# Ones-matmuls one slice later, attention tails in three steps, SGU steps strewn: one change to a hybrid decoder layer on eight NeuronCores

## The chip, the cores, the metric

One Trainium2 chip, all 8 cores. Cores 2b and 2b+1 compute sequence b of four: the even core its first 1116 positions, the odd core the other 932, for which it also builds keys and values of the first 1024 positions (the context stage). No core waits for another. SGU is the spatial gating unit, adaLN the conditioning by c. The metric is the device time of one execution in microseconds (us), that is of the slowest core.

Such a program has a second, slower state: one die (cores 0 to 3 or 4 to 7), or both, shows a lower granted TensorE clock. Slow runs are not compared here. Beside fast runs I use the spans of **odd cores on undisturbed dies**: dies whose two even cores both lie within 0.2% of the lowest even core of that kernel's runs.

## The reference, cut

```python
mod = silu(c) @ w_ada + b_ada                    # adaLN: shift, scale, gate, twice
h = rms(x, norm1_g) * (1 + scale1) + shift1
zu, zv, zq, zk, zvb, za, zb = split(h @ w_in)
y_a = gelu(zu) * (w_s @ rms(gelu(zv)) + b)       # SGU, in 128-position chunks, 16 groups
# y_b: 16 heads, two 128-wide q/k components each, v of 256
q, k = rms(q, q_norm_g), rms(k, k_norm_g)        # QK norm
p = softmax(q @ k.T * 128**-0.5 - slope * dist, causal)
o = (p[:, :, 0] - lam * p[:, :, 1]) @ v
y_b = rms(o, subln_g) * (1 - lambda_init)
x = x + gate1 * ((sigmoid(za) * y_a + sigmoid(zb) * y_b) @ w_out)
x = x + gate2 * conv_ffn(rms(x, norm2_g) * (1 + scale2) + shift2)
# ... shapes, spatial gating and ConvFFN cut
```

## The kernel before

The program of each engine is fixed when the kernel is built: `P.pe`, `P.act`, `P.dve`, `P.pool` and `P.op("sp", ...)` append to five lists, and semaphore waits follow from the buffers that are named. An engine executes its list in order, so what is emitted first is done first. A projection (`spec_F`, or `spec_T` for V) is a chain of groups of 32 accumulating matmuls, cut into four **slices** of eight; after each slice `bg.slice()` runs what was put off (`later`) and then, at a given rate, the next steps of attention and SGU.

```python
class Bg:
    def __init__(self):
        self.q, self.rate, self.credit, self.pend, self.now = deque(), 0.0, 0.0, deque(), 0
        self.gate, self.open = set(), True

    def slice(self):
        self.now += 1
        while self.pend and self.pend[0][0] <= self.now:
            self.pend.popleft()[1]()
        self.credit += self.rate
        while self.credit >= 1.0:
            self.credit -= 1.0
            if self.q:
                if self.gate and self.q[0] in self.gate and not self.open:
                    self.credit += 1.0
                    break
                self.q.popleft()()

    def later(self, fn, n=1):
        self.pend.append((self.now + n, fn))
# ...
def gemm(bk, m, n, lhs, rhs, rd, evict):

    for g in range(NG):
        P.pe([(lambda e, kc=kc, a=lhs(kc), b=rhs(kc): e.matmul(bk.v[0:m, 0:n], lhsT=a, rhs=b, start=(kc == 0), stop=(kc == FC - 1)))
              for kc in range(g * KS, (g + 1) * KS)], reads=rd(g), writes=[bk.b], acc=True)
        if g == NG - 1:
            evict(bk)
        yield
```

The QK norm: square the group's result on ScalarE, sum over partitions with a matmul by ones, then rsqrt (Ln, Exp) and scale. `later` with its default of 1 is reached in the very `bg.slice()` that follows the group, so the ones-matmul stands directly behind the group's last matmul. The sigmoids of the gates have a first and a second half too:

```python
def qknorm(sqr, tmr, gname, dst, dbuf):
    def ev(bk, n):
        q, _ = sqr.next()
        P.act(lambda e: e.activation(out=q.v[:, 0:n], in_=bk.v[:, 0:n], func=AF.Square), reads=[bk.b], writes=[q.b])

        def rest():
            sb = srow.next()
            P.pe(lambda e: e.matmul(sb.v[:, 0:n], lhsT=ones_b.v, rhs=q.v[:, 0:n], start=True, stop=True),
                 reads=[q.b, ones_b.b], writes=[sb.b])
            r, _ = tmr.next()
            ln_exp(sb.v[:, 0:n], r.v[:, 0:n], sb.b, r.b, 1.0 / 128)
            P.dve(lambda e: e.scalar_tensor_tensor(out=dst, in0=bk.v[:, 0:n], scalar=cc(gname), in1=r.v[:, 0:n], op0=ALU.mult, op1=ALU.mult),
                  reads=[bk.b, r.b, cst.b], writes=[dbuf], acc=True)
        bg.later(rest)
    return ev
# ...
def ev_sig(dst):
    def f(bk, l, r0, n):
        t, _ = tmr.next()
        tv = t.v[:, 0:n]
        P.act(lambda e: e.activation(out=tv, in_=bk.v[:, 0:n], func=AF.Exp, scale=-1.0), reads=[bk.b], writes=[t.b])
        P.dve(lambda e: e.tensor_scalar_min(out=tv, in0=tv, scalar1=EMAX), writes=[t.b])

        def rest():
            P.act(lambda e: e.activation(out=tv, in_=tv, func=AF.Ln, bias=onec, scale=1.0), reads=[cst.b], writes=[t.b])
            P.act(lambda e: e.activation(out=dst.v[:, l, r0 - OFF:r0 - OFF + n], in_=tv, func=AF.Exp, scale=-1.0),
                  reads=[t.b], writes=[dst.b], acc=True)
        bg.later(rest)
    return f
```

Attention of a head, in steps (**units**): for each pair of query block and key block `qk` (scores, exponential) and, `LAG` steps later, `pv` (accumulate P times V and the row sums in two banks, `acc`). After a block's last pair its tail (`tail1`), and four steps later the transposes (`tail2`):

```python
def qk(p, j, kb, nk):
    a, b = qcols[j]
    nq, kn = b - a, krows(kb)
    sb = srow.next()
    P.pe([(lambda e, cm=cm: e.matmul(sb.v[0:kn, cm * nq:(cm + 1) * nq], lhsT=K.v[:, cm, kb * 128:kb * 128 + kn],
                                     rhs=Q.v[:, cm, a - OFF:b - OFF], start=True, stop=True)) for cm in range(2)],
         reads=krd + [Q.b], writes=[sb.b])
    pt, _ = pTr.next()
    bi = h * c.NBMAX + (NC + j - kb)
    P.act(lambda e: e.activation(out=pt.v[0:kn, 0:2 * nq], in_=sb.v[0:kn, 0:2 * nq], func=AF.Exp, bias=cc("albi", bi)[0:kn], scale=SC),
          reads=[sb.b, cst.b], writes=[pt.b])
    if kb == nk - 1:
        o = a - blocks[j][0]
        P.dve(lambda e: e.tensor_tensor(out=pt.v[0:kn, 0:2 * nq].rearrange("p (a b) -> p a b", a=2),
                                        in0=pt.v[0:kn, 0:2 * nq].rearrange("p (a b) -> p a b", a=2),
                                        in1=tri[0:kn, None, o:o + nq].to_broadcast([kn, 2, nq]), op=ALU.mult),
              reads=[msk.b], writes=[pt.b])
    pts[p] = pt

def pv(p, j, kb, nk):
    a, b = qcols[j]
    nq, kn = b - a, krows(kb)
    pt = pts.pop(p)
    P.pe([(lambda e, cm=cm: e.matmul(acc[cm].v[0:nq, 0:257], lhsT=pt.v[0:kn, cm * nq:(cm + 1) * nq], rhs=V.v[0:kn, kb, 0:257],
                                     start=(kb == 0), stop=(kb == nk - 1))) for cm in range(2)],
         reads=vrd + [pt.b], writes=[acc[0].b, acc[1].b], acc=True)

ohs = {}

# ...
def tail1(j):
    nq = qcols[j][1] - qcols[j][0]
    oa, _ = oar.next()
    oh, _ = ohr.next()
    ohs[j] = oh
    x = j % 2
    rr, rs = sm_rr[x][0:nq], sm_rs[x][0:nq]
    P.act(lambda e: e.activation(out=oa.v[0:nq, 0, 0:257], in_=acc[0].v[0:nq, 0:257], func=AF.Copy), reads=[acc[0].b], writes=[oa.b])
    P.dve(lambda e: e.tensor_copy(out=oa.v[0:nq, 1, 0:257], in_=acc[1].v[0:nq, 0:257]), reads=[acc[1].b], writes=[oa.b])
    P.dve(lambda e: e.reciprocal(out=rr[:, :, None], in_=oa.v[0:nq, :, 256:257]), reads=[oa.b], writes=[B_rr[x]])
    P.dve(lambda e: e.tensor_scalar_mul(out=rr[:, 1:2], in0=rr[:, 1:2], scalar1=neglam.v[0:nq]),
          reads=[neglam.b], writes=[B_rr[x]])
    P.dve(lambda e: e.tensor_scalar_mul(out=oa.v[0:nq, 1, 0:256], in0=oa.v[0:nq, 1, 0:256], scalar1=rr[:, 1:2]),
          reads=[B_rr[x]], writes=[oa.b])
    P.dve(lambda e: e.scalar_tensor_tensor(out=oa.v[0:nq, 0, 0:256], in0=oa.v[0:nq, 0, 0:256], scalar=rr[:, 0:1], in1=oa.v[0:nq, 1, 0:256],
                                           op0=ALU.mult, op1=ALU.add), reads=[B_rr[x]], writes=[oa.b])
    P.act(lambda e: e.activation(out=jk.v[0:nq], in_=oa.v[0:nq, 0, 0:256], func=AF.Square, accum_out=rs), reads=[oa.b], writes=[jk.b, B_rs[x]])
    P.act(lambda e: e.activation(out=rs, in_=rs, func=AF.Ln, bias=epsc[0:nq], scale=1.0 / 256), reads=[cst.b], writes=[B_rs[x]])
    P.act(lambda e: e.activation(out=rs, in_=rs, func=AF.Exp, scale=-0.5), writes=[B_rs[x]])
    P.act(lambda e: e.activation(out=oh.v[0:nq, 0, :], in_=oa.v[0:nq, 0, 0:256], func=AF.Identity, scale=rs),
          reads=[oa.b, B_rs[x]], writes=[oh.b])
    P.dve(lambda e: e.scalar_tensor_tensor(out=oh.v[0:nq, 1, :], in0=oa.v[0:nq, 0, 0:256], scalar=rs, in1=oh.v[0:nq, 0, :],
                                           op0=ALU.mult, op1=ALU.subtract), reads=[oa.b, B_rs[x]], writes=[oh.b])

def tail2(j):
    a, b = qcols[j]
    nq = b - a
    oh = ohs.pop(j)
    sb = srow.next()
    P.pe([(lambda e, e2=e2, w=w: e.matmul(sb.v[:, e2 * nq:(e2 + 1) * nq], lhsT=oh.v[0:nq, w, e2 * 128:(e2 + 1) * 128], rhs=ident[0:nq, 0:nq],
                                          start=(w == 0), stop=(w == 1))) for e2 in range(2) for w in range(2)],
         reads=[oh.b, msk.b], writes=[sb.b])
    P.dve([(lambda e, e2=e2: e.tensor_scalar_mul(out=oT.v[:, e2, a - OFF:b - OFF], in0=sb.v[:, e2 * nq:(e2 + 1) * nq],
                                             scalar1=subc.v[:, e2:e2 + 1])) for e2 in range(2)],
          reads=[sb.b, subc.b], writes=[oT.b], acc=True)

for p, (j, kb, nk) in enumerate(pairs):
    ev[p].append(lambda p=p, j=j, kb=kb, nk=nk: qk(p, j, kb, nk))
    ev[p + LAG].append(lambda p=p, j=j, kb=kb, nk=nk: pv(p, j, kb, nk))
    if kb == nk - 1:
        ev[p + LAG].append(lambda j=j: tail1(j))
        ev[p + LAG + 4].append(lambda j=j: tail2(j))
out = []
for s in sorted(ev):
    out.append(lambda fs=ev[s]: [f() for f in fs])
return out
```

The loop over heads (scores, ones sums, tails and SGU take turns in three banks, `srow`; projections have three others, `mainb`):

```python
for h in range(H):
    last = h == H - 1
    load_sgu(h)
    if not last:
        load_ctx(h + 1)
    bg.rate = 0.0
    run(spec_F(("u", h), hb, hf.otiles, mainb, ev_u)); run_ada()
    bg.q.extend(attn_units(h))
    gated = sgu_units(h)
    bg.q.extend(gated)
    bg.gate, bg.open = set(gated), False
    if not last:
        bg.q.append(lambda h=h: y_unit(h))
    bg.spread(2 * NF + (0 if last else NF + NFK + NT_), 0.8 if last else 1.0)
    run(spec_F(("gb", h), hb, hf.otiles, mainb, ev_sig(sB))); run_ada()
    run(spec_F(("ga", h), hb, hf.otiles, mainb, ev_sig(sA)))
    bg.later(open_gate)
    if last:
        bg.flush_pend()
    run_ada()
    if not last:
        run(spec_F(("k", h + 1), hb, hf.xtiles, mainb, ev_qk(h + 1, "k"))); run_ada()
        run(spec_T(("v", h + 1), hb, blocks, mainb, ev_v(h + 1))); run_ada()
        run(spec_F(("q", h + 1), hb, hf.otiles, mainb, ev_qk(h + 1, "q"))); run_ada()
        bg.flush()
```

In the context stage of the odd cores, while keys and values of the context are projected, background steps load the core's own x and sum its squares; each loads what it uses itself (`own_build`, which normalises x in a second pass, does the same):

```python
def own_stat(ti, k0):
    (r0, n) = hf.xtiles[ti]
    xv, xb = xl1.load(osrc[ti], k0, n)
    for i in range(2):
        if k0 + i == 0:
            P.act(lambda e, i=i: e.activation(out=rst1[ti].v, in_=xv[i], func=AF.Square), reads=[xb[i]], writes=[rst1[ti].b])
        else:
            P.act(lambda e, i=i: e.activation(out=xv[i], in_=xv[i], func=AF.Square), writes=[xb[i]])
            P.pool(lambda e, i=i: e.tensor_tensor(out=rst1[ti].v, in0=rst1[ti].v, in1=xv[i], op=ALU.add), reads=[xb[i]], writes=[rst1[ti].b])
```

Of the kernel before, what the change touches and what calls it, by code (L numbers as in the profile page):

```python
# [78 lines left out]
class Prog:  # L79
# [12 lines left out]
    dsem = sem  # L92
# [272 lines left out]
def build(cfg):  # L365
# [20 lines left out]
    kT_s = scr("kT_s", [H, 128, 2, CMAX])  # L386
# [6 lines left out]
    with ExitStack() as st:  # L393
# [10 lines left out]
        def emit(P, hf):  # L404
            A = Arena(arena_t[:, :], AB)
            pb = [Bank(psum[i], i) for i in range(8)]
            bg = Bg()
            T, R, OFF, NC, NBLK, NKB = hf.T, hf.R, hf.OFF, hf.NC, hf.NBLK, hf.NKB
            blocks = [(128 * j, min(128, R - 128 * j)) for j in range(NBLK)]
            qcols = [(max(OFF, r0), r0 + n) for (r0, n) in blocks]  # L410
# [92 lines left out]
            def run(gen):  # L503
                for _ in gen:
# [6 lines left out]
                  reads=[cst.b], writes=[lamw.b])  # L511
# [170 lines left out]
# [10 lines that stand above are left out]
                        ln_exp(sb.v[:, 0:n], r.v[:, 0:n], sb.b, r.b, 1.0 / 128)  # L692
                        P.dve(lambda e: e.scalar_tensor_tensor(out=dst, in0=bk.v[:, 0:n], scalar=cc(gname), in1=r.v[:, 0:n], op0=ALU.mult, op1=ALU.mult),  # L693
                              reads=[bk.b, r.b, cst.b], writes=[dbuf], acc=True)
                    bg.later(rest)
                return ev

            Bkv_s = [[Buf(f"kv_s{h}.{i}") for i in range(4)] for h in range(H)]
            if NC:
                A.next_phase(off_h0 + FC * hf.C * 2)  # L700
                rst1 = [A.alloc(f"rso{i}", [128, n], F32) for i, (_, n) in enumerate(hf.xtiles)]
                kst = Ring(P, A, "kst", 2, [128, hf.C], BF16, dma=True)
                vst = Ring(P, A, "vst", 2, [128, NC // 2, 256], BF16, dma=True)
                sqb1 = Ring(P, A, "sqb", 1, [128, c.TW], BF16)
                tm1 = Ring(P, A, "tm", 1, [128, c.TW], F32)
                xl1 = XLoad("xo", 2, 2, max(n for _, n in hf.xtiles))
                h1 = HBuf("hown", hf.xtiles, R, TOP1)
                mainb = Banks(pb, [0, 1, 2, 3, 4])
# [11 lines that stand above are left out]
                def own_fin(ti):  # L720
                    n = hf.xtiles[ti][1]
                    sb = srow.next()
                    P.pe(lambda e: e.matmul(sb.v[:, 0:n], lhsT=ones_f.v, rhs=rst1[ti].v, start=True, stop=True),
                         reads=[rst1[ti].b, ones_f.b], writes=[sb.b])
                    ln_exp(sb.v[:, 0:n], rst1[ti].v, sb.b, rst1[ti].b, 1.0 / D)

                def own_build(ti, k0):
                    xv, xb = xl1.load(osrc[ti], k0, hf.xtiles[ti][1])
                    for i in range(2):
                        build_h(h1, ti, k0 + i, xv[i], xb[i], rst1[ti])  # L730
                for ti in range(len(hf.xtiles)):
                    for k0 in range(0, FC, 2):
                        bg.q.append(lambda ti=ti, k0=k0: own_stat(ti, k0))
                bg.q.append(lambda: None)
                for ti in range(len(hf.xtiles)):
                    bg.q.append(lambda ti=ti: own_fin(ti))
                for ti in range(len(hf.xtiles)):
                    for k0 in range(0, FC, 2):
                        bg.q.append(lambda ti=ti, k0=k0: own_build(ti, k0))
                bg.spread(int(0.8 * H * NG * (2 * len(hf.ctiles) + NC)))  # L740
                cblk = [(128 * j, 128) for j in range(NC)]

                def ctx_head(h):
                    cur = {}

                    def evk(bk, l, r0, n):
                        if r0 == 0:
                            cur[l] = kst.next()
                        t, s = cur[l]
                        qknorm(sqb1, tm1, "kg", t.v[:, r0:r0 + n], t.b)(bk, n)  # L750
                        if r0 + n == hf.C:
                            bg.later(lambda: P.op("sp", lambda e: e.dma_start(out=kT_s[h][:, l, 0:hf.C], in_=t.v), reads=[t.b], writes=[Bkv_s[h][l]], dsem=s))

                    def evv(bk, j, n):
                        hv = NC // 2
                        if j % hv == 0:
                            cur["v"] = vst.next()
                        t, s = cur["v"]
                        P.dve(lambda e: e.tensor_copy(out=t.v[:, j % hv, :], in_=bk.v[:, 0:256]), reads=[bk.b], writes=[t.b], acc=True)
                        if j % hv == hv - 1:  # L760
                            P.op("sp", lambda e: e.dma_start(out=vB_s[h][:, j - hv + 1:j + 1, :], in_=t.v), reads=[t.b],
                                 writes=[Bkv_s[h][2 + j // hv]], dsem=s)
                    run(spec_F(("kc", h), h0, hf.ctiles, mainb, evk))
                    run_ada()
                    run(spec_T(("vc", h), h0, cblk, mainb, evv))
                    run_ada()
                for h in range(H):
                    ctx_head(h)
                bg.flush()
                hb = h1  # L770
            else:
                hb = h0
# [107 lines left out]
            def ev_sig(dst):  # L880
                def f(bk, l, r0, n):
# [5 lines left out]
                    def rest():  # L887
                        P.act(lambda e: e.activation(out=tv, in_=tv, func=AF.Ln, bias=onec, scale=1.0), reads=[cst.b], writes=[t.b])
                        P.act(lambda e: e.activation(out=dst.v[:, l, r0 - OFF:r0 - OFF + n], in_=tv, func=AF.Exp, scale=-1.0),
                              reads=[t.b], writes=[dst.b], acc=True)  # L890
                    bg.later(rest)
                return f

            def attn_units(h):
# [1 line left out]
                K, Q, V = Ks[i], Qs[i], Vs[i]  # L896
                krd = [Kc[i][1]] + ([Kc[i][0]] if NC else [])
                vrd = [Vc[i][1], Vc[i][2]] + ([Vc[i][0]] if NC else [])
                LAG = 2
                ev = defaultdict(list)  # L900
                pts = {}
                pairs = []
# [33 lines left out]

                ohs = {}

                def tail1(j):
                    nq = qcols[j][1] - qcols[j][0]  # L940
                    oa, _ = oar.next()
                    oh, _ = ohr.next()
                    ohs[j] = oh
                    x = j % 2
                    rr, rs = sm_rr[x][0:nq], sm_rs[x][0:nq]
                    P.act(lambda e: e.activation(out=oa.v[0:nq, 0, 0:257], in_=acc[0].v[0:nq, 0:257], func=AF.Copy), reads=[acc[0].b], writes=[oa.b])  # L946
                    P.dve(lambda e: e.tensor_copy(out=oa.v[0:nq, 1, 0:257], in_=acc[1].v[0:nq, 0:257]), reads=[acc[1].b], writes=[oa.b])  # L947
                    P.dve(lambda e: e.reciprocal(out=rr[:, :, None], in_=oa.v[0:nq, :, 256:257]), reads=[oa.b], writes=[B_rr[x]])
# [3 lines left out]
                          reads=[B_rr[x]], writes=[oa.b])  # L952
                    P.dve(lambda e: e.scalar_tensor_tensor(out=oa.v[0:nq, 0, 0:256], in0=oa.v[0:nq, 0, 0:256], scalar=rr[:, 0:1], in1=oa.v[0:nq, 1, 0:256],  # L953
                                                           op0=ALU.mult, op1=ALU.add), reads=[B_rr[x]], writes=[oa.b])
                    P.act(lambda e: e.activation(out=jk.v[0:nq], in_=oa.v[0:nq, 0, 0:256], func=AF.Square, accum_out=rs), reads=[oa.b], writes=[jk.b, B_rs[x]])  # L955
                    P.act(lambda e: e.activation(out=rs, in_=rs, func=AF.Ln, bias=epsc[0:nq], scale=1.0 / 256), reads=[cst.b], writes=[B_rs[x]])
                    P.act(lambda e: e.activation(out=rs, in_=rs, func=AF.Exp, scale=-0.5), writes=[B_rs[x]])
# [2 lines left out]
                    P.dve(lambda e: e.scalar_tensor_tensor(out=oh.v[0:nq, 1, :], in0=oa.v[0:nq, 0, 0:256], scalar=rs, in1=oh.v[0:nq, 0, :],  # L960
                                                           op0=ALU.mult, op1=ALU.subtract), reads=[oa.b, B_rs[x]], writes=[oh.b])

                def tail2(j):
                    a, b = qcols[j]
                    nq = b - a
                    oh = ohs.pop(j)
# [8 lines left out]
                for p, (j, kb, nk) in enumerate(pairs):  # L975
                    ev[p].append(lambda p=p, j=j, kb=kb, nk=nk: qk(p, j, kb, nk))
                    ev[p + LAG].append(lambda p=p, j=j, kb=kb, nk=nk: pv(p, j, kb, nk))
                    if kb == nk - 1:
                        ev[p + LAG].append(lambda j=j: tail1(j))
                        ev[p + LAG + 4].append(lambda j=j: tail2(j))  # L980
                out = []
                for s in sorted(ev):
                    out.append(lambda fs=ev[s]: [f() for f in fs])
# [71 lines left out]
            for h in range(H):  # L1055
# [3 lines left out]
                    load_ctx(h + 1)  # L1059
                bg.rate = 0.0  # L1060
                run(spec_F(("u", h), hb, hf.otiles, mainb, ev_u)); run_ada()
                bg.q.extend(attn_units(h))
                gated = sgu_units(h)
                bg.q.extend(gated)
                bg.gate, bg.open = set(gated), False
                if not last:
                    bg.q.append(lambda h=h: y_unit(h))
                bg.spread(2 * NF + (0 if last else NF + NFK + NT_), 0.8 if last else 1.0)
                run(spec_F(("gb", h), hb, hf.otiles, mainb, ev_sig(sB))); run_ada()
                run(spec_F(("ga", h), hb, hf.otiles, mainb, ev_sig(sA)))  # L1070
                bg.later(open_gate)
                if last:
                    bg.flush_pend()
                run_ada()
# [332 lines left out]
```

## Time and profile before

| | before |
|---|---|
| runs | 9843.2, 9851.55 (fast), 11061.12 us (slow); median 9851.55 |
| span, core 1 / core 0 (undisturbed die of the profiled execution, itself slow) | 9846.4 / 9344.4 us |
| core 1: context stage and the SGU's gate input, to the first attention scores | 0 to 2256 us |
| core 1: attention stage, to the first matmul of w_out | 2256 to 6124 us |
| core 1: w_out and FFN | 6124 to 9846 us |
| core 1: TensorE's waits in the attention stage | 570 us |
| core 1: heads' distance, with / without adaLN tiles | 252 / 241 us |

How to read it: the slowest kind of core sets the time, so the odd cores; on them the engine that is full where it can be, so TensorE; on it the waits, and the clock. The lines are in the prediction.

### The profile page before, as it was taken

How to read it: one execution, taken by the hardware profiler on the slowest of the kernel's cores; microseconds unless marked ns; L12 is line 12 of the kernel's file. 1: busy time of each engine (PE TensorE's matmuls, PEld its weight loads, DVE VectorE, ACT ScalarE, POOL GpSimd, SP SyncE). 2: the span in 40 equal slices, each digit the busy share in tenths (PEclk: the TensorE clock that was granted, in tenths of full speed). 3: DMA queues.
4: the chain of work that ended last, by engine and by line, in shares of the span. 5: the costliest groups of instructions: out<-in, count | busy, mean ns of one | idle time of the engine just before them, and what ended most of it. 6: DMA issues, size and time to landing. Idle time of an engine off the chain costs nothing.

```text
span 10025.4 us, 141616 instructions; the slowest of 8 cores (9343.0 to 10025.4 us)
## 1 busy us (share of the span) xinstructions
PE 8931.1 (89%) x56778; PEld 5043.5 (50%) x56778; DVE 1854.3 (18%) x3461; ACT 2023.2 (20%) x4331; POOL 770.3 (8%) x1051
## 2 busy tenths in 40 slices
PE   4188789998888888888888888999999999999999
PEld 2155457875555555555555544444444444444444
DVE  0101110001111111111111111133444334300000
ACT  1121111223333333333333332100000000000000
POOL 0011000000000000000000001100000000011111
PEclk8599999999999999999999999999999999988888
DMA  9966656563344444333233325655555555466555
GB/s 195 190 142 138 135 120 123 122 130 85 79 85 84 85 85 83 77 65 65 60 61 67 61 47 132 157 104 117 119 114 107 107 110 111 109 130 98 92 93 90
DMA packets 216618, 1045.06 MB, mean 104 GB/s; under 512 B 22176, under 2 KB 99616, under 8 KB 169120
## 3 DMA queue, kind: packets, MB, share of 16 engines
q0 software_dynamic: 99936, 807.45, 44.7%
q1 hardware_dynamic: 116032, 228.44, 7.1%
q8 instruction: 470, 7.70, 0.3%
q14 instruction: 180, 1.47, 0.1%
HBM read 1759.77 MB, written 83.43 MB: 184 GB/s over the span
## 4 chain that ended last, share of the span: by engine, by line
PE 81%; DMA 6%; ACT 5%; issue 3%; DVE 3%; SPq 0%; another core or an unknown queue 0%; POOL 0%; ACTq 0%; DVEq 0%; POOLq 0%
PE pb L646 60%; PE pb L1308 12%; PE pb L933 4%; DMA arena<-xt 4%; DMA arena<-w_ada 2%; PE pb L914 2%; ACT arena L685 1%; PE pb L488 1%; ACT arena L919 1%; PE pb L689 1%; PE pb L611 1%; ACT arena L955 1%; DVE arena L953 1%; DVE arena L947 1%; ACT arena L946 0%
## 5 line engine op out<-in xcount | busy, mean ns | idle before, releaser
L646 PE MATMUL pb<-arena 128*128 128x467 bf16 (+3 forms) x37504 | 6831.0, 339 | 13.8 <-DMA arena<-w_in 10.3
L646 PEld LDWEIGHTS pb<-arena 128*128 128x128 bf16 x37504 | 3640.7, 99 | 2659.8 <-issue 127.6
L1308 PE MATMUL pb<-arena 128*128 128x466 bf16 x5504 | 1278.3, 404 | 4.0 <-DMA arena<-act_s 3.0
L1308 PEld LDWEIGHTS pb<-arena 128*128 128x128 bf16 x5504 | 588.0, 107 | 694.3 <-issue 7.8
L933 PE MATMUL pb<-arena 128*128 128x257 bf16 (+1 forms) x3200 | 640.9, 286 | 323.9 <-ACT arena L919 257.1
L919 ACT ACTIVATE arena<-pb,arena 128x256 bf16<-128x256 f32 (+1 forms) x1600 | 693.7, 455 | 972.8 <-PE pb L914 971.3
L933 PEld LDWEIGHTS pb<-arena 128*128 128x128 bf16 (+1 forms) x3200 | 280.2, 100 | 558.1 <-issue 439.1
L1207 ACT ACTIVATE arena<-arena 128x932 f32<-128x932 f32 x86 | 84.4, 982 | 2096.4 <-DVE arena L1204 2096.4
L1188 DVE TENSOR_TENSOR arena<-pb,arena 128x467 f32<-128x467 f32 x344 | 221.9, 645 | 1260.1 <-PE pb L646 1260.1
L914 PE MATMUL pb<-arena 128*128 128x128 bf16 (+1 forms) x3200 | 451.1, 224 | 0.0
L1204 DVE SCALAR_TENSOR_TENSOR arena<-arena 128x932 f32<-128x932 f32 x344 | 409.5, 1190 | 36.1 <-DVE arena L1201 0.5
L315 POOL DMA_DIRECT2D arena<-w_in x144 | 79.2, 550 | 4211.9 <-PE pb L646 2184.7
L689 PE MATMUL pb<-arena 128*128 128x512 bf16 (+1 forms) x192 | 75.3, 392 | 359.3 <-ACT arena L685 359.3
L693 DVE SCALAR_TENSOR_TENSOR arena<-pb,arena 128x512 bf16<-128x512 f32 (+1 forms) x192 | 141.3, 736 | 1214.7 <-ACT arena L525 1208.1
L914 PEld LDWEIGHTS pb<-arena 128*128 128x128 bf16 x3200 | 313.5, 102 | 89.5 <-issue 30.8
L488 PE MATMUL pb<-arena 128*128 128x1 bf16 x6144 | 172.3, 164 | 186.5 <-DMA arena<-w_ada 186.5
L488 PEld LDWEIGHTS pb<-arena 128*128 128x128 bf16 x6144 | 171.1, 98 | 207.6 <-issue 202.0
L315 POOL DMA_DIRECT2D arena<-w_down x352 | 185.7, 528 | 1154.5 <-PE pb L1308 1142.2
L1293 DVE SCALAR_TENSOR_TENSOR arena<-pb,arena 128x466 f32<-128x466 f32 x64 | 45.0, 703 | 1237.0 <-PE pb L1308 1057.4
L685 ACT ACTIVATE arena<-pb 128x512 bf16<-128x512 f32 (+1 forms) x192 | 111.8, 582 | 802.4 <-PE pb L646 802.4
L689 PEld LDWEIGHTS pb<-arena 128*128 128x128 bf16 x192 | 18.5, 96 | 446.9 <-issue 446.9
L611 PE MATMUL pb<-arena 128*128 128x512 f32 x128 | 113.0, 1018 | 118.4 <-ACT arena L607 60.6
(93 smaller groups left out, 3012.1 us busy)
## 6 DMA issues: line engine op xcount, KB each, us to landing
arena<-w_in POOLq DMA_DIRECT2D x144, 2048.0 KB, 14.3
arena<-w_ada POOLq DMA_DIRECT2D x96, 2048.0 KB, 25.0
arena<-w_up POOLq DMA_DIRECT2D x86, 2048.0 KB, 14.8
arena<-w_down POOLq DMA_DIRECT2D x320, 256.0 KB, 4.0
arena<-xt SPq DMA_DIRECT2D x64, 512.0 KB, 9.1
arena<-w_out POOLq DMA_DIRECT2D x16, 2048.0 KB, 15.4
arena<-xt SPq DMA_DIRECT2D x24, 1024.0 KB, 27.3
act_s<-arena SPq DMA_DIRECT2D x86, 233.0 KB, 9.8
```

Source lines behind the costliest of these rows:

```text
L315: self.P.pool(lambda e, dst=dst, src=src: e.dma_start(out=dst, in_=src), writes=[t.b], dsem=s)
L488: P.pe([(lambda e, kc=kc, l=l: e.matmul(bk.v[:, l:l + 1], lhsT=wv[:, kc, l * 128:(l + 1) * 128], rhs=scb.v[:, kc:kc + 1], start=(kc == 0), ...
L611: P.pe(lambda e, qv=qv, i=i: e.matmul(bk.v[:, 0:n], lhsT=ones_f.v, rhs=qv, start=(k0 + i == 0), stop=(k0 + i == FC - 1)), reads=[qb, ones_ ...
L646: P.pe([(lambda e, kc=kc, a=lhs(kc), b=rhs(kc): e.matmul(bk.v[0:m, 0:n], lhsT=a, rhs=b, start=(kc == 0), stop=(kc == FC - 1))) for kc in r ...
L685: P.act(lambda e: e.activation(out=q.v[:, 0:n], in_=bk.v[:, 0:n], func=AF.Square), reads=[bk.b], writes=[q.b])
L689: P.pe(lambda e: e.matmul(sb.v[:, 0:n], lhsT=ones_b.v, rhs=q.v[:, 0:n], start=True, stop=True), reads=[q.b, ones_b.b], writes=[sb.b])
L914: P.pe([(lambda e, cm=cm: e.matmul(sb.v[0:kn, cm * nq:(cm + 1) * nq], lhsT=K.v[:, cm, kb * 128:kb * 128 + kn], rhs=Q.v[:, cm, a - OFF:b - ...
L919: P.act(lambda e: e.activation(out=pt.v[0:kn, 0:2 * nq], in_=sb.v[0:kn, 0:2 * nq], func=AF.Exp, bias=cc("albi", bi)[0:kn], scale=SC), read ...
L933: P.pe([(lambda e, cm=cm: e.matmul(acc[cm].v[0:nq, 0:257], lhsT=pt.v[0:kn, cm * nq:(cm + 1) * nq], rhs=V.v[0:kn, kb, 0:257], start=(kb == ...
L1188: P.dve(lambda e: e.tensor_tensor(out=tgt.v[:, PAD + t0:PAD + t0 + n], in0=bk.v[:, 0:n], in1=rs2.v[:, t0:t0 + n], op=ALU.mult), reads=[bk. ...
L1204: P.dve(lambda e, jj=jj: e.scalar_tensor_tensor(out=dst.v, in0=tgt.v[:, jj:jj + TO], scalar=cw(jj), in1=dst.v, op0=ALU.mult, op1=ALU.add), ...
L1308: P.pe([(lambda e, kc=kc, o=bks[ccg][ti].v[:, 0:nn], a=wv[:, kk, :], b=acts[kc].v[:, t0:t0 + nn]: e.matmul(o, lhsT=a, rhs=b, start=(kc == ...
```

## The change

The intent is to keep TensorE from waiting behind ScalarE: put instructions later where their inputs are not yet there, and keep ScalarE's queue free of instructions that would stand and wait.

```diff
@@ qknorm: @@
                         P.dve(...)
-                    bg.later(rest)
+                    bg.later(rest, 2)
@@ context stage, store of K: @@
-                            bg.later(lambda: P.op("sp", ...kT_s...))
+                            bg.later(n=2, fn=lambda: P.op("sp", ...kT_s...))
@@ ev_sig: @@
-                    bg.later(rest)
+                    bg.later(rest, 2)
@@ attn_units: @@
-                LAG = 2
+                LAG = 3
-                def tail1(j):
+                def tail_o(j):          # copy of acc, VectorE's chain
 ...
+                def tail_n(j):          # Square, Ln, Exp, Identity, last subtraction
 ...
-                def tail2(j):
+                def tail_t(j):          # transposes
 ...
-                        ev[p + LAG].append(lambda j=j: tail1(j))
-                        ev[p + LAG + 4].append(lambda j=j: tail2(j))
+                        ev[p + LAG].append(lambda j=j: tail_o(j))
+                        ev[p + LAG + 3].append(lambda j=j: tail_n(j))
+                        ev[p + LAG + 6].append(lambda j=j: tail_t(j))
@@ loop over heads: @@
-                bg.q.extend(attn_units(h))
-                gated = sgu_units(h)
-                bg.q.extend(gated)
+                att, gated = attn_units(h), sgu_units(h)
+                if last:
+                    att += gated
+                else:
+                    a = len(att) // 2
+                    step = (len(att) - a) // len(gated)
+                    for i, u in enumerate(gated):
+                        att.insert(a + i * (step + 1), u)
+                bg.q.extend(att)
 ...
-                bg.later(open_gate)
+                bg.later(open_gate, 2)
```

The bodies of the tails are the old ones, cut in two (the cuts in the diff are marked by dots). With `later(..., 2)` one more slice of eight matmuls, and the units after it, stand between a group and its ones-matmul.

## The prediction

> **What bounds the kernel now.** I read the list of cores first, because the printed page is of core 7, on a die in its slow state (clock 0.937). The time of a fast run (9843 and 9851 us; the third, 11061, is slow) is that of a second-half core on the other die:
>
> ```profile
> core 0: 9344.4 us, clock 0.965
> core 1: 9846.4 us, clock 0.956
> core 2: 9343.0 us, clock 0.965
> core 3: 9847.5 us, clock 0.956
> ...
> ```
>
> Odd cores hold the second half of a sequence and do 100 attention pairs per head, even ones 45. So I read core 1 throughout. Its page, in 40 slices of 246 us:
>
> ```profile
> PE   4188789998888888888888887999999999999999
> ACT  1111111223333333333333333210000000000000
> PEclk8599899999999999999999998999999999999999
> ```
>
> TensorE is the bound: from slice 26 on (w_out, FFN) it is full; from slice 9 to 25 (attention, one head after another) it is busy at "8" while ScalarE is at "3". By the stretches view the attention stage (2250 to 6200 us) has TensorE busy some 430 of each 500 us at a granted clock of 0.95, against 500 of 500 at 1.00 in the FFN. That missing share is all that a reordering can win. Next, who ends TensorE's idle time: the waits of TensorE in 2250 to 6200 us (microseconds in all, times, longest), then in 560 to 2150 us, the context stage:
>
> ```profile
> PE pb L933 <- ACT arena L919: 257.5, 156, 3.5
> PE pb L689 <- ACT arena L685: 183.4, 120, 4.0
> PE pb L933 <- DVE arena L947: 62.7, 65, 3.3
> PE pb L1007 <- DVE arena L1000: 51.5, 19, 5.9
> PE pb L968 <- DVE arena L960: 9.2, 2, 5.4
> ...
> PE pb L689 <- ACT arena L685: 168.8, 62, 15.7
> ```
>
> L933 is P times V, waiting for the exponentials of L919; L689 is the ones-matmul of the QK norm, waiting for the squares of L685; L1007 is the SGU. With two strays of 3 us they make 570 us in attention and 169 in context. After 6200 us TensorE waits 6 us in all: nothing to win. Last, the timeline around a block's end shows why L919 is late:
>
> ```profile
> 3155.56 0.39 ACT L946 ACTIVATE arena<-pb 128x257 f32<-128x257 f32 x1 [0.58 <-PE pb L933]
> 3158.21 0.42 ACT L955 ACTIVATE arena<-arena 128x256 bf16<-128x256 f32 x1 [2.27 <-DVE arena L953]
> 3159.49 0.51 ACT L958 ACTIVATE arena<-arena 128x256 bf16<-128x256 f32 x1
> 3159.90 0.82 ACT L919 ACTIVATE arena<-pb,arena 128x256 bf16<-128x256 f32 x2
> 3160.50 0.59 PE L933 MATMUL pb<-arena 128*128 128x257 bf16 x2 [2.51 <-ACT arena L919]
> 3161.74 1.91 PE L646 MATMUL pb<-arena 128*128 128x256 bf16 x8
> 3164.18 1.05 PE L646 MATMUL pb<-arena 128*128 128x256 bf16 x8
> ```
>
> The whole tail of a block stands ahead of the next exponential in ScalarE's queue. ScalarE copies the accumulator, idles 2.27 us for VectorE's chain (L947 to L953), does the norm, and reaches the exponential 4.3 us after the copy; TensorE has by then waited 2.51 us. The last two rows are the same eight matmuls: 1.91 us just after the wait, 1.05 us shortly afterwards. Waiting also costs clock.
>
> **What the Trainium skill says.** "TensorE: Matmul & The Clock Gate", section "What's actually happening": after about 3.4 us of idleness the clock is halved and is given back after as long a busy stretch. The trace agrees in kind: 1.91 against 1.05. Its section "Architectural detail" calls the ScalarE and VectorE queues strictly first in, first out; the 4.3 us above are that. Its section "Seeing it yourself" says to budget 1.95 GHz for dense matmul on all cores. The trace of the undisturbed die disagrees: clock 1.00 with TensorE 500 of 500 us busy. So I do not let a denser attention stage be throttled. [...] I count waits and slice durations, not busy shares.
>
> **The change part by part**, for core 1. No arithmetic is added or removed; the order of instructions shows the same matmuls moved. A slice is eight matmuls: on the timeline 1.58 us at 467 columns, 1.73 at 512, 0.89 at 256; an attention unit (two L933, two L914) adds 0.33.
>
> *Ones-matmul later.* Now it is issued straight behind its group, and waits 0.95 us even with ScalarE free (square 0.58 plus two hand-overs). With the new argument one more slice and its unit stand between, 1.2 to 2.1 us. In attention 120 waits are mostly 0.92 to 1.02, with a few of 3.7 behind block tails that the split removes: 183 us go to about nothing. In context some 45 of the 62 waits are about 1 us and vanish; 17 are 1.4 to 15.7 us, where ScalarE sits behind loads of x, and only lose 1.7 us each. 45 + 29 = 74; since a faster TensorE runs into the same loads sooner, I credit 66. Sum: 249.
>
> *Tails in three steps and LAG 3.* The norm comes three units after the copy, 3.7 us in the fastest stage (1.22 per unit) against about 2.4 for VectorE's chain, so ScalarE's 2.27 us stall (294 us over 128 blocks) ends, and its work between two exponentials falls from 4.3 to about 1.8 us. P times V now follows its scores by three units, at least 2.5 us even where two units share a slice, against 0.8 for a free exponential and 1.9 behind the norm. The wait goes in heads 0 to 14: 257.5 - 28 (last head, added from the timeline) = 229. In the last head 2.8 units share each slice, and of its 28 I take 15 away. Three banks hold scores, ones sums, transposes and SGU; scores of unit s wait at worst for exponential s-2, over 1.5 us old by then. Sum: 244.
>
> *SGU strewn.* The scaled weights (L1000) are made some six units before use: of 51.5 us the 42 outside the last head go. In the last head the SGU stays at the end.
>
> *Left as it is.* L933 waiting for L947: the accumulators must be copied before the next block, 1.53 us from one to the other; the new order has, per head, two block ends with the next unit in the same slice, one of them behind a ones-matmul: some 3.6 us per head, as now.
>
> *Clock.* Heads take 252 us (the first eight, with adaLN tiles) and 241 (the others; distances between like waits). Warm work, counted by slices: 64 x 1.58 + 16 x 1.73 + 32 x 0.89 + 100 x 0.33 + 8 for small matmuls = 198, plus 5 for adaLN. With 35 us of waits, 14 and 8 us per head are left: half speed. 8 x 14 + 7 x 8 = 168, and a few in the last head. With waits of at most 2.6 us left alone, I take back 150.
>
> Together 249 + 244 + 42 + 150 = 685 us. 9851 - 685 = 9166; I say 9160. Heads would take about 210 and 203 us. Even cores have 0.97 in clock and 259 us of ones-matmul waits to gain from 9344, so they stay below 9100 and don't set the time.
>
> **The rivals.** (1) The wait moves: the norm's sum and the exponentials share ScalarE and three banks, so L914 could wait for banks, or L933 for L947, since a 0.45 us SGU scaling on VectorE (four in a row) can stand before the accumulator's copy. For: L914's idle time is 0.0 now only because L933 takes the wait first. Against: ScalarE is busy 37% in this stage and VectorE 17%. If half of the 244 returned, with half the clock: 9360. (2) Weight loads become the bound. Heads move about 84 GB/s at 252 us, the context stage 130; at 208 us a head needs about 102. Against it. In context it is partly true, and taken off above; if all of that gain were lost, 9225. (3) The clock gate is not about waits: adaLN's one-column matmuls may keep it cold, or the denser stage is throttled. Then 100 of the 150 stay: 9260.
>
> **Range and chances.** Rival (2) and half of (3) together give about 9280, everything hidden and all clock returned about 9090. I take 9070 to 9290. Two per cent is 9654: it would need over two thirds of the 685 to come back, which no row supports: 0.96 faster, 0.03 same, 0.01 slower.
>
> **What would show it.** Right: on core 1, L689 under 20 us of waits in attention and about 100 in context; ScalarE's wait for L953 under 30 us; L933 for L919 under 30; L947 near 60; clock 0.99 in the attention stage; FFN unchanged. Wrong: L914 or L933 with new waits of over 100 us for L919, L971 or L947; weight loads named as releasers of L646; or clock still 0.95 without waits, which would part the clock from the idling.

## The result, and the profile after

| | before | after |
|---|---|---|
| runs | 9843.2, 9851.55, (11061.12) | 9119.26, 9122.4, (9288.35) us |
| odd cores, undisturbed dies, mean (range) | 9837 (9824 to 9866; 24 dies, runs beside the experiments) | 9114 (9082 to 9149; 14 dies, both series) |
| even cores, the same dies, mean | 9346 | 8864 |
| core 1: start to first scores | 2256 | 2159 us |
| core 1: attention stage | 3868 | 3201 us |
| core 1: w_out and FFN | 3722 | 3724 us |

In brackets: slow. The ratio is 0.9262, with a 95% interval of 0.9222 to 0.9302: faster. Ratios here are the mean time of one kernel's fast runs over that of the other's of the same rounds, so not quite the ratio of the medians quoted. A second series on another chip gave 0.9326 (0.9229 to 0.9423); of its three fast runs one, 9256, has a die with odd cores up to 9254 at a clock of 0.959, so it is less clean.

The list of cores of the changed kernel (span, mean granted clock), then core 1's page rows, in 40 slices of 227 us:

```profile
core 0: 8865.6 us, clock 0.974
core 1: 9084.1 us, clock 0.976
core 2: 8861.9 us, clock 0.974
core 3: 9115.1 us, clock 0.973
```

```profile
PE   5179789999999999999999989999999999999999
...
ACT  1112121223444444444444431100000000000000
...
PEclk8589899999999999999999999999999999999999
```

The attention stage (now slices 9 to 23) has gone from "8" to "9" on TensorE, and its clock, 0.95 by the stretches view before, is 1.00. ScalarE went from "3" to "4": the same work in less time. The waits of TensorE on core 1, in 2150 to 5560 us, then (last line) in the context stage, 560 to 2150 us (us in all, times, longest). Line numbers have shifted: L946 was L947, L975 was L968 (the transposes), L967 was L960, L1015 and L1008 are the SGU:

```profile
PE pb L933 <- DVE arena L946: 47.2, 35, 2.6
PE pb L975 <- DVE arena L967: 39.4, 16, 5.4
PE pb L1015 <- DVE arena L1008: 9.7, 3, 5.9
...
PE pb L933 <- ACT arena L919: 0.7, 3, 0.3
...
PE pb L689 <- ACT arena L685: 108.0, 15, 20.2
```

All rows of the attention stage sum to 107 us, against 570. The two large ones are gone: P times V waits 0.7 us for exponentials (257.5), the ones-matmul not at all (183.4). One row is new in size: the transposes' wait for the norm's last step, 9 before, 39 now. And the context stage still has 108 us, in 15 waits instead of 62 (cores 3, 5 and 7 of this run: 118.5, 134.4 and 108.7).

What came back besides waits shows in the stretches view of core 1, from the first scores to w_out, before and then after (stretch, length, busy time and count of TensorE, its weight loads, VectorE, ScalarE, GpSimd; granted clock, DMA share, GB/s):

```profile
2256.00:6124.00 3868.00, 3296.57 (x22387) 1947.27 (x22386) 670.85 (x1770) 1433.19 (x3203) 311.57 (x332) 0.95 0.36 74
...
2159.00:5360.00 3201.00, 3093.79 (x22382) 1882.86 (x22381) 655.06 (x1770) 1407.35 (x3203) 309.54 (x332) 1.00 0.43 89
```

For the same matmuls (the counts differ by a few at the borders) TensorE is busy 203 us less, at a clock of 1.00 instead of 0.95. These and the 463 us of waits make up the 667 us by which the stage got shorter.

Why the exponential is no longer late shows at a block's end, on the timeline of core 1 (start, duration, engine and line, in brackets the idle time before and its releaser). I took the block end with the largest wait that is left:

```profile
3097.25 0.37 ACT L945 ACTIVATE arena<-pb 128x257 f32<-128x257 f32 x1
...
3098.11 0.41 DVE L946 COPY arena<-pb 128x257 f32<-128x257 f32 x1
...
3098.67 0.38 PE L933 MATMUL pb<-arena 128*128 128x257 bf16 x2 [2.56 <-DVE arena L946]
...
3099.06 1.05 PE L646 MATMUL pb<-arena 128*128 128x256 bf16 x8
...
3100.91 0.41 ACT L962 ACTIVATE arena<-arena 128x256 bf16<-128x256 f32 x1
...
3102.18 0.51 ACT L965 ACTIVATE arena<-arena 128x256 bf16<-128x256 f32 x1
...
3102.60 0.86 ACT L919 ACTIVATE arena<-pb,arena 128x256 bf16<-128x256 f32 x2
```

L962, the norm's square (L955 before), starts without a bracket: nothing was waited for, where 2.27 us stood before. From it to the exponential are 1.7 us, and P times V of those exponentials comes three units on and does not wait. The 2.56 us are the wait for the accumulator copy that was left as it is, at a block end with a ones-matmul's Ln and Exp before it and the next unit in the same slice. It comes once per head in the first eight heads. After it the eight matmuls take 1.05 us: full speed.

### The profile page after: what moved, and what is told of

The parts are those of the page before. It is cut to its first block, busy times and chain, and to the rows that moved or that the text cites. A ratio compares the mean times of both kernels' runs of the same rounds, so it can differ in the third digit from the quotient of the medians.

```text
span 9120.4 us, 141419 instructions; the slowest of 8 cores (8860.8 to 9120.4 us)
## 1 busy us (share of the span) xinstructions
PE 8530.5 (94%) x56778; PEld 4925.4 (54%) x56778; DVE 1840.0 (20%) x3461; ACT 1997.5 (22%) x4331; POOL 768.8 (8%) x1051
## 4 chain that ended last, share of the span: by engine, by line
PE 88%; DMA 7%; ACT 1%; DVE 1%; issue 1%; SPq 1%; another core or an unknown queue 0%; ACTq 0%; DVEq 0%; POOL 0%; POOLq 0%
PE pb L646 67%; PE pb L1322 11%; DMA arena<-xt 5%; PE pb L933 4%; PE pb L914 2%; DMA arena<-w_ada 2%; PE pb L488 1%; PE pb L611 1%; PE pb L689 1%; SPq L1255 0%; DMA arena<-w_in 0%; PE pb L975 0%; PE pb L1156 0%; DVE arena L946 0%; DVE arena L565 0%
## 5 line engine op out<-in xcount | busy, mean ns | idle before, releaser
L646 PE MATMUL pb<-arena 128*128 128x467 bf16 (+3 forms) x37504 | 6715.9, 335 | 12.0 <-DMA arena<-w_in 10.6
L646 PEld LDWEIGHTS pb<-arena 128*128 128x128 bf16 x37504 | 3600.0, 98 | 2614.9 <-issue 57.6
L1322 PE MATMUL pb<-arena 128*128 128x466 bf16 x5504 | 1092.9, 360 | 6.5 <-DMA arena<-act_s 5.4
L1322 PEld LDWEIGHTS pb<-arena 128*128 128x128 bf16 x5504 | 535.6, 97 | 563.7 <-issue 8.9
L933 PE MATMUL pb<-arena 128*128 128x257 bf16 (+1 forms) x3200 | 601.2, 273 | 48.4 <-DVE arena L946 47.1
L914 PE MATMUL pb<-arena 128*128 128x128 bf16 (+1 forms) x3200 | 430.8, 216 | 4.6 <-DVE arena L1025 2.5
L933 PEld LDWEIGHTS pb<-arena 128*128 128x128 bf16 (+1 forms) x3200 | 278.8, 97 | 254.4 <-issue 103.2
L914 PEld LDWEIGHTS pb<-arena 128*128 128x128 bf16 x3200 | 298.0, 97 | 85.4 <-issue 39.4
L488 PEld LDWEIGHTS pb<-arena 128*128 128x128 bf16 x6144 | 171.1, 98 | 208.7 <-issue 203.2
```

The lines of the kernel that those rows point to most:

```text
L488: P.pe([(lambda e, kc=kc, l=l: e.matmul(bk.v[:, l:l + 1], lhsT=wv[:, kc, l * 128:(l + 1) * 128], rhs=scb.v[:, kc:kc + 1], start=(kc == 0), ...
L1322: P.pe([(lambda e, kc=kc, o=bks[ccg][ti].v[:, 0:nn], a=wv[:, kk, :], b=acts[kc].v[:, t0:t0 + nn]: e.matmul(o, lhsT=a, rhs=b, start=(kc == ...
```

## The experiments

Twelve runs. The table gives odd cores on undisturbed dies, against 9837 for the kernel before and 9114 for the changed one.

| run | what | odd cores, mean (dies) | fast runs, us |
|---|---|---|---|
| e5 | late ones-matmuls alone | 9673 (4) | 9693.9 |
| e2 | tails in three, LAG 3, alone | 9411 (3) | 9418.9, (9472.9) |
| e3 | SGU strewn, alone | 9722 (6) | 9732.1, 9734.2 |
| e4 | change, tail in one piece | 9305 (6) | 9344.9 |
| e6 | change, LAG 2 | 9167 (4) | 9189.5 |
| e10 | change, sigmoids as before | 9202 (9) | 9210.1, 9217.9, (9345.7) |
| e7 | change + loads one unit ahead | 8967 (4) | 8981.8, (9082.0) |
| e8 | change + empty steps kept | 9055 (6) | 9073.3, (9149.7) |
| e11 | e7 + e8 | 8908 (8) | 8911.7, 8912.2, 8914.4 |
| e12 | e11 + split copies | 8897 (9) | 8897.5, 8909.9, 8911.8 |

Fast runs in brackets have one die at a lower clock than the others. All outputs were correct.

### e1, e5: the late ones-matmuls alone

```diff
--- before
-                    bg.later(rest)          # in qknorm
+                    bg.later(rest, 2)
-                            bg.later(lambda: ...kT_s...)
+                            bg.later(n=2, fn=lambda: ...kT_s...)
```

> The kernel before with the ones-matmuls of the QK norm (and the K store behind them) two slices late, nothing else. Theory 1, each part removes its own waits and the clock comes back in proportion: TensorE's waits of the ones-matmul for the squares on core 1 fall from 183 to about 50 us in attention (the ones of 3.7 us behind a block's tail only shrink) and from 169 to about 110 in context, the waits of P times V stay near 257; the time falls by 200 to 300 us, to 9550-9650. Theory 2, the parts hide each other (a late ScalarE holds up squares and exponentials alike): the wait moves to P times V, which goes over 330 us, and the time falls by under 120 us.

e1's five executions were all slow (10433 to 10897 us; clocks from 0.82), so it decided nothing and was run again:

> The same kernel as in the first experiment (late ones-matmuls alone), whose runs all fell in the slow state, so that the same numbers are expected: theory 1 (each part removes its own waits), 200 to 300 us below the kernel before, ones-matmul waits about 50 us in attention and 110 in context, waits of P times V near 257; theory 2 (the parts hide each other), under 120 us and P times V over 330. Since tails alone gave some 400 us and SGU alone 108, theory 1 wants close to 210 here for the parts to add up to the whole 720.

One fast run, 9693.9 us; odd cores 164 us below the kernel before. TensorE's waits on core 1 in attention, from the run's trace:

```profile
PE pb L933 <- ACT arena L919: 269.8, 167, 3.4
...
PE pb L968 <- DVE arena L960: 63.7, 16, 5.4
...
PE pb L689 <- ACT arena L685: 20.7, 8, 2.6
```

The ones-matmul's own wait fell from 183 to 21 us, more than expected, and in context from 169 to 78. P times V rose by 12 only, so the wait did not move there. But the transposes, 9 before, took 64: once per head, behind its last scores, they now wait for the tail's last step. So the gain of 164 lies between the theories' numbers, nearer to the first: the part removes its own waits, and some 55 us of them went to the transposes while the tails were still in one piece. The other half of theory 1, that the clock comes back in proportion, failed: attention got 97 us shorter on core 1, its waits 98, and TensorE stayed busy 3297 us in it, as before. Of the 120 waits before, 88 were about 1 us long; in place of the 22 of about 3.7 stand the transposes' 16, nearly all of 3.8. That the short ones cost no clock would fit this; it is not shown apart.

### e2: the tails alone

```diff
--- before
-                LAG = 2
+                LAG = 3
 # and tail_o, tail_n, tail_t with their steps, as in the change
```

> The kernel before with the tails in three steps and LAG 3, nothing else. Theory 1: the waits of P times V for exponentials fall from 257 us to under 30, the long ones of the ones-matmul (3.7 us) go too, so that it waits about 120 in attention, SGU waits stay near 50; the granted clock in attention rises from 0.95 to 0.98 or more; the time falls by 380 to 480 us, to 9370-9470. Theory 2, what is hidden behind this part alone is nearly all: the time falls by over 550 us, to under 9300.

9418.9 us, odd cores 426 us below: theory 1. The waits on core 1:

```profile
PE pb L689 <- ACT arena L685: 134.3, 125, 2.3
PE pb L933 <- DVE arena L946: 77.1, 82, 3.3
...
PE pb L933 <- ACT arena L919: 3.0, 3, 2.2
```

The exponentials' wait is gone, the long waits of the ones-matmul went with it (longest 2.3, was 4.0), and the clock from 2250 to 5000 us rose from 0.95 to 0.99. In e5, with P times V's wait left in place, it stayed at 0.95. From the first scores to w_out TensorE was busy 3150 us instead of 3297 for the same matmuls: this part alone brought 146 of the 203 us of clock back.

### e3: the strewn SGU alone

```diff
--- before
-                bg.q.extend(attn_units(h)); gated = sgu_units(h); bg.q.extend(gated)
+                ... the nine SGU steps inserted into the second half of att, as in the change
```

> The kernel before with the SGU steps strewn among the attention steps of every head but the last, nothing else. Theory 1: the SGU's waits for its scaled weights fall from 51 us to about 10, the rest stays; the time falls by 40 to 70 us. Theory 2: the scaling on VectorE stands before the accumulator copies and P times V waits over 40 us more for them, so that the time does not fall (within 20 us).

Two fast runs, 9732 and 9734 us: 115 us on odd cores where 40 to 70 were expected. The wait for the scaled weights fell from 51.5 to 9.7 as expected, and no other grew by more than 3 us; the wait for the accumulator copies stayed (62.7, now 62.2). The ones-matmul lost 25 us more, probably because the block tails fall elsewhere between the groups (not shown); 44 us came without waits: TensorE was busy 3252 us in the attention stage instead of 3297, at a clock of 0.96 instead of 0.95. The direction of theory 1 holds; its size was too small by half.

The three parts alone give 164 + 426 + 115 = 705 us; the whole gives 723. But the whole has the sigmoid part too, which none of the three has: without it (e10) the three together give 635 us, 70 less than their sum. So they do not simply add; where they overlap was not tested.

### e4, e6: the split or the lag

```diff
--- after (e4)
-                        ev[p + LAG + 3].append(lambda j=j: tail_n(j))
-                        ev[p + LAG + 6].append(lambda j=j: tail_t(j))
+                        ev[p + LAG].append(lambda j=j: tail_n(j))
+                        ev[p + LAG + 4].append(lambda j=j: tail_t(j))
--- after (e6)
-                LAG = 3
+                LAG = 2
```

> The changed kernel with the tail in one piece again (copy, VectorE chain and norm in one step, transposes four steps on), LAG 3, late ones-matmuls and strewn SGU kept. Theory 1, the split is what frees ScalarE: its wait for VectorE's chain is again near 290 us, P times V waits 60 to 130 us for exponentials (mostly where V is projected, units 1.22 us apart), and the time is 100 to 200 us above the changed kernel's. Theory 2, LAG 3 alone hides the stall: within 50 us of the changed kernel.

> The changed kernel with P times V two units behind its scores again, as before, all else changed. Theory 1, the split of the tail is what counts: after the norm an exponential is done about 1.9 us after its scores and P times V comes 2.2 us after them where V is projected, so only units that share a slice wait, under 1 us: 10 to 40 us of waits and the time 10 to 50 us above the changed kernel's. Theory 2, the longer lag is what counts: over 100 us.

e4, with the tail in one piece, lost 190 us; e6, with the shorter lag, 53. In e4 ScalarE's wait for VectorE's chain was back at 295.4 us, and these rows of an undisturbed core (5) are the exponentials', 117 us together:

```profile
PE pb L914 <- ACT arena L919: 79.8, 53, 2.6
...
PE pb L933 <- ACT arena L919: 36.7, 24, 3.0
```

L914, the scores, waits for exponentials here because they have to leave one of three banks: this is the rival of the prediction in which the wait moves to L914, and a lag of 3 alone runs into it. In e6 P times V waited 26.7 us in 50 waits. So the split is the larger half, as theory 1 has it; the lag was worth slightly more than the 50 us allowed for.

### e10 (with e9, the changed kernel again): the sigmoids

```diff
--- after
-                    bg.later(rest, 2)       # in ev_sig
+                    bg.later(rest)
```

> The changed kernel itself, unchanged, beside the next three and the kernel before: fast runs of 9100 to 9140 us, a ratio of 0.92 to 0.93 to the kernel before. If the chip of these runs differs from that of the first comparison, this is the base for the next three.

> The changed kernel with the second half of the sigmoids issued at once again (one slice instead of two), all else changed. Theory 1: ScalarE is not the bound there and has 3 units of lag to spare, so that its stalls of 0.6 us for VectorE (80 us in all before) come back without moving the end: within 15 us of the changed kernel. Theory 2: they delay exponentials and accumulator copies, and P times V waits over 40 us more: over 40 us slower.

e9 gave fast runs of 9150.7, 9175.4 and 9256.0 us, odd cores 9116 on nine undisturbed dies, beside 9111 in the first series: the base stands. e10 was 86 us above it, ratio 0.9415 (0.9252 to 0.9579) to the kernel before. My theory 1 fell. ScalarE's own stalls of 0.6 us, 81 us in all, do delay what stands behind them:

```profile
PE pb L933 <- DVE arena L946: 76.2, 51, 3.3
...
PE pb L914 <- ACT arena L919: 15.3, 9, 2.0
```

With the sigmoids late these are 47.2 and 0.6; the rows are almost those of e2 (77.1 and 15.5), which has the early sigmoids too. So 44 us of waits came back in these two rows, for 86 us of time. The other half is slower matmuls: from the first scores to w_out TensorE was busy 3138 us, for those that took 3094 in the changed kernel.

### e7: what is left in the context stage

```diff
--- after
+                xq = deque((ti, k0) for _ in range(2) for ti in ... for k0 in range(0, FC, 2))
+                xgot = deque()
+                def xnext():
+                    while xq and len(xgot) < 2:
+                        ti, k0 = xq.popleft()
+                        xgot.append(xl1.load(osrc[ti], k0, hf.xtiles[ti][1]))
+                    return xgot.popleft()
-                    xv, xb = xl1.load(osrc[ti], k0, n)      # own_stat
+                    xv, xb = xnext()
-                    xv, xb = xl1.load(...)                  # own_build
+                    xv, xb = xnext()
```

The reason to try it, from the timeline of the changed kernel, core 1 (SPq is the queue of SyncE, which issues these transfers in order):

```profile
639.93 0.33 SPq L752 DMA_DIRECT2D kT_s<-arena  x1
640.51 0.33 SPq L548 DMA_DIRECT2D arena<-xt  x1
...
648.23 1.15 ACT L717 ACTIVATE arena<-arena 128x512 f32<-128x512 f32 x2 [9.23 <-DMA arena<-xt]
...
650.26 0.59 PE L689 MATMUL pb<-arena 128*128 128x512 bf16 x1 [5.97 <-ACT arena L685]
```

The load of x is issued 0.6 us after the K store that stands before it in the queue, and that store has to wait for normalised keys: SyncE had issued nothing since 621.3. ScalarE stands 9.2 us for the load; behind it in its queue stands the square that the ones-matmul needs.

> The changed kernel, with the loads of x in the context stage put in the queue one unit ahead of their use (two buffers as before). Theory 1, what is left of the ones-matmul's wait there (108 us on core 1) comes of loads that stand in the queue behind the K stores and are issued only when they are needed: the wait falls under 30 us and the time by 60 to 120 us. Theory 2, the loads are late because the DMA engines are shared with 2 MB weight tiles: the wait stays over 80 us and the time within 25 us.

Odd cores fell by 147 us, best run 8981.8. The wait in context:

```profile
PE pb L689 <- ACT arena L685: 4.0, 2, 3.1
```

108 to 4 us: theory 1. The gain is larger than the 60 to 120 expected. The loads themselves got slower, not faster: from issue to landing 11.1 us in the median of this stage, 7.6 before. So it was their late issue that cost time; e7 does not part the wait behind the store from a load that is asked for only when it is needed.

### e8: the transposes' new wait

```diff
--- after
-                for s in sorted(ev):
+                for s in range(max(ev) + 1):
                     out.append(lambda fs=ev[s]: [f() for f in fs])
```

> The changed kernel, with empty steps kept in the list of attention steps, so that the last block of a head too has three steps between copy, norm and transposes (they follow at one step now, since empty steps are left out). Theory 1: the new wait of the transposes for the norm's last step (39 us on core 1, 2.2 us per head) falls under 15 us, and the time by 20 to 45 us. Theory 2, the wait only moves to the end of the head (flush, next head): within 10 us.

The distances 3 and 6 are between keys of `ev`; behind a head's last pair most keys have no entry and are left out, so that copy, norm and transposes follow one after the other. Before the change this hardly mattered. The changed kernel's timeline at the end of a head:

```profile
5208.41 3.35 PE L646 MATMUL pb<-arena 128*128 128x467 bf16 x16
...
5214.24 0.38 PE L975 MATMUL pb<-arena 128*128 128x128 bf16 x4 [2.49 <-DVE arena L967]
```

With the empty steps kept, the wait is 5.4 us in one place (the last head; core 1, on an undisturbed die) instead of 39.4 in 16, and odd cores fell by 59 us, against an expected 20 to 45. Theory 1. The surplus: the accumulator copies' wait fell too, from 47.2 to 31.1, its longest from 2.6 to 1.3.

### e11, e12: put together

```diff
--- e11 (e12)
+            oab = [t.bufs(2) for t in oar.t]      # a buffer of its own for each half of oa
-  ACT copy writes oa.b; DVE copy writes oa.b
+  ACT copy writes o0;   DVE copy writes o1        # and the later steps name o0, o1
```

> The changed kernel with the loads of x one unit ahead and the empty steps kept, both together. They cure different waits in different stages, so that they should add: 138 and 47 us in the single runs, 160 to 200 us together, to 8920-8970 us, about 0.91 of the kernel before. Against it: a slower addition if the even cores, near 8850, or the die's variation set the time.

> As the combined kernel, with the two accumulator copies of a block's end on two buffers, so that VectorE's copy no longer waits for ScalarE's. Theory 1: the chain from the last P times V to the next block's first one gets 0.5 us shorter (1.53 to about 1.05 us), its wait falls from 31 us on core 1 to under 15, and the time falls by 10 to 30 us more. Theory 2: the wait is set by VectorE being late for other reasons: no change within 8 us.

e11 (e7 and e8 together) ran at 8911.7 to 8914.4 us: ratio 0.904 (0.8987 to 0.9093) to the kernel before. Its odd cores are 206 us below the changed kernel, which is just 147 + 59. In e12 the wait for the accumulator copies was still

```profile
PE pb L943 <- DVE arena L957: 20.3, 27, 1.3
```

on core 5, an undisturbed one (31.1 on core 1 of e11), not under 15, and odd cores fell by 11 us more; fast runs 8897.5 to 8911.8, ratio 0.9035 (0.8996 to 0.9073). Odd cores say theory 1, a little; the times of the two kernels overlap, so at the level of whole runs it is not settled. e11 and e12 beat both kernels. Their even cores stand at 8849 us, so only some 50 us are left before these set the time.

## Why the prediction was right, point by point

The prediction was 9160 us, 9070 to 9290, faster; measured 9122.

- **The odd cores' TensorE waits are what the change can win**: right. w_out and FFN took 3722 and 3724 us.
- **Ones-matmul, 249 us.** The attention part went as written, 183 to nothing (though the waits of about 3.7 us, "a few" there, were 22 of the 120). In context 108 us stay, 100 were forecast. Core 1 reaches its first scores 97 us earlier, of which 7 were gained before the first context matmul; 66 was credited. From that matmul on its waits for squares fell by 68 us and TensorE's busy time, for the same 12628 matmuls, by 22. In attention this part alone gave no clock back (e5).
- **Tails and LAG 3, 244 us.** 257.5 to 0.7. The last head, of whose 28 us I took only 15 off, keeps some 6, now mostly at the transposes. ScalarE's wait for VectorE's chain, forecast under 30, is 34.4. e4 and e6 confirm the mechanism and its two halves. (One reading was loose: when the exponential starts, TensorE has waited 1.9 us; 2.51 is the whole wait.)
- **SGU, 42 us**: 51.5 to 9.7, as written; alone it gave more (e3).
- **Left as it is: L933 for L947**, forecast about 60: 47. The single wait of 2.6 us at one block end per head was read off the order of instructions, and is there at 2.56. But the sum stayed low for a reason that the prediction lacks: **the late sigmoids, which it did not price at all**. e10 shows them worth 86 us and this wait 76 without them.
- **Clock, 150 us**: too small. The attention stage got 667 us shorter, its waits 463; the other 203 are busy time of the same matmuls, of which the tails alone gave 146, the SGU 44 and the ones-matmuls none. The 0.99 forecast is 1.00. Heads now lie 208 and 202 us apart, for 210 and 203 forecast.
- **Rival 1**, the wait that moves, came true in a row that it did not name: the transposes, 39 us, and removing it gave 59 (e8). Scores waiting more than 3 us in all for exponentials to leave their banks were seen only in e2, e4 and e10. **Rival 2**: weight loads did not bind in attention (89 GB/s there by the stretches view, at TensorE waits of 107 us, none on a weight load); in context it was loads of x, late by their issue rather than by bandwidth (e7). **Rival 3** did not come true: the clock came back with the waits. But not with every wait: in e5 98 us of them went and no clock came back.

The terms were each too small or too large by some tens of us, and those too small (clock, context, sigmoids) outweigh the transposes that were overlooked: 38 us in all. That they cancel so far is luck. Core 1 itself gained 762 us, 77 more than the sum; but it is the fastest odd core of its run (9084 us), and the slowest, at 9120, sets the time.

## What to carry to other kernels

In an in-order queue an instruction that waits is worse than one that comes late: move it behind work that is ready, and look for what stands behind it. Count the distance in what really lies between, not in step numbers: empty steps, several steps per slice and rotating banks shorten it. And price a wait on TensorE above its length when it is long: before the change those of over 2.2 us mostly had matmuls at half speed behind them, the shorter ones seldom (the counts are in the next section). The tails' waits cost about 0.5 us more for each us (e2: 146 us of busy time with 275 of waits), the ones-matmul's alone nothing (e5: none with 98, new long waits at the transposes included).

## What the Trainium skill lacked or had wrong

- "TensorE: Matmul & The Clock Gate", section "What's actually happening", gives the idle window as about 3.4 us. On core 1 before, of the waits of P times V of 2.2 to 2.7 us, 31 of 40 were followed by P times V at half speed (over 0.5 us for two, 0.38 warm), over 2.7 us 17 of 20, under 2.2 us 9 of 163. After the change 1 of 8 of those of 2.2 to 2.7. What else decides in that range the runs do not show.
- The same page, section "Seeing it yourself", says to budget 1.95 GHz for dense matmul on all cores. Undisturbed dies granted 1.00 with TensorE busy 500 of 500 us on their cores. A lower clock came and went with the run: whole-run means down to 0.80 on one die beside 0.97 on the other. Where it held, the figure fits the page's 13/16: in e1, from 7000 to 7500 us, all eight cores had 0.81 or 0.82. But on core 1 it was 1.00 from 8000 to 9000 us of the same run, with TensorE busy 500 of 500 us. So that clock comes and goes here under dense matmul; what selects it is not shown.
- No page spells out what it costs when a load stands behind a waiting store in the issuing engine's queue: "DMA: Bandwidth & Descriptors", section "Issuing engines are not separate DMA queues", speaks of the shared engines. Here issuing the loads one unit earlier gained 147 us (e7).
